# Attention scores from two 128-row matmuls, and running products times differences of values

## The chip, the cores and the metric

The kernel runs on one core of one Trainium2 chip. The metric is the device time of one execution in microseconds; before the change it is 1440.06 us (median of three runs, 1440.01 to 1440.62).

## What is computed

One decoder block over 1024 tokens of width 1024, all in float32: a norm and one wide input projection; two token mixers (an attention without softmax, and a gated linear attention, GLA); their gated merge and output projection; a gated feed-forward net with a short convolution; a last norm. The change lies in the attention, which has 8 heads of 64:

```python
z = einsum('bhqd,bhkd->bhqk', qb, kb) * scale          # scale = 64 ** -0.5
strict = s_idx < t_idx
log_keep = where(strict, log_sigmoid(-z), 0.0)
tail = cumsum(log_keep, reverse=True) - log_keep       # over the keys right of s
w = where(strict, exp(log_sigmoid(z) + tail), 0.0)
out = einsum('bhqk,bhkd->bhqd', w, vb)
```

In words: for a query t, each key s < t has a share b = sigmoid(z) and keeps 1 - b = sigmoid(-z). The weight of s is its b times the product of what all keys between s and t keep. With K(s) the product of sigmoid(-z) over the keys from s up to t - 1 (and K = 1 from t on), the weight of s is K(s + 1) - K(s).

## The kernel before

Matrix products in float32 are made of matmuls in a rounded type (fp32r): each operand is split into a high part, rounded, and a low part, the rest, by the helper `split` (line 118): a cast on ScalarE (ACT, line 119) and a subtraction on VectorE (DVE, line 110). `mac` (line 189) multiplies high by high, high by low and low by high; its matmuls have line 195. DVE's products have line 113 and its sums line 116, as these too are helpers.

The order of the instructions on each engine is set when the kernel is built: a scheduler takes the program's instructions by priority, which is their order in the program, when their inputs and buffers are ready by its own model of time. All engines work through their queues in order. Tiles come from pools with a fixed number of buffers: `t8` (128 x 2048, 16 buffers), `t4` (128 x 1024, 14), `t2` (128 x 512, 11), and 8 PSUM banks of 128 x 512.

The projections of the queries and keys lie in DRAM as `sqk_d` (a row for each of the 512 query and 512 key channels, a column for each token), the values as `sbv_d` (a row for each token).

`attend` (line 670) goes over four pairs of heads (j), over four groups of 256 queries (tp), over the two heads of the pair (e), over the two blocks of 128 queries in the group (i), and over the keys up to the block in chunks of at most 512 (four blocks of 128), the rightmost chunk first. That is 96 chunks in all. Each chunk goes through three steps, with up to six chunks queued between the first and the second:

- `weigh` (line 623): scores z of 128 queries by up to 512 keys in two matmuls. The first (line 631) has 128 rows: the high part of the 64 query channels and their low part below it, against the high part of the keys, doubled. The second (line 632) has 64 rows: the high part of the queries against the low part of the keys. ACT then makes sigmoid(z) (`be`, line 634) and sigmoid(-z) (`ke`, line 635). In a block's first chunk, GpSimd (POOL) masks both on the diagonal (line 638); in the others it multiplies the last column of `be` by the product that the chunk to the right left (line 643). DVE makes the running product of `ke` from the right (a scan, line 646), and multiplies `be` by it, moved by one column (line 648, seen as line 113).
- `turn_weights` (line 651): transposes the weights `be` in blocks on TensorE (line 654) and splits them.
- `gather` (line 657), when a group of queries is through: the values, in high and low parts side by side in 128 columns, times the weights' parts (line 663). The two halves of the result are added (a copy on ACT, line 666, and a sum on DVE), and the sum is stored to `osb_d` from SyncE's queue (SP).

`qk(j, t)` (line 562) prepares a pair: 11 loads on SP's queue, then in four steps the casts (lines 578 and 581) and subtractions (579 and 582). Pair 0 is prepared ahead of `attend`; the next pair from the last group of queries (tp = 3) of the current one on, a step after each chunk. `value_blocks` (line 613) loads and splits the value blocks in pairs during pair 0.

In between stand the matmuls of the merge gates (`gates`, line 524, seen as line 195). They need nothing from the attention; they have a lower priority, and `fill` hands out a step of six after every 3.6 key blocks or so.

Of the kernel before, what the change touches and what calls it, by code (L numbers as in the profile page):

```python
# [3 lines left out]

# [6 lines left out]
F32 = mybir.dt.float32  # L11
F32R = mybir.dt.float32r
AF = mybir.ActivationFunctionType
ALU = mybir.AluOpType
# [3 lines left out]
P = 128  # L18
D = 1024
S = 1024  # L20
NT = S // P
NK = D // P
HALF = 512
SBH, SBD = 8, 64
# [41 lines left out]
def block_kernel(ctx: ExitStack, tc: tile.TileContext, x, norm_mix_g, w_in, b_gate, w_alpha_up, b_alpha,  # L66
# [20 lines left out]
    def t8(dt=F32R):  # L87
        return sb.tile([P, 2 * D], dt, tag="t8", name=nm("t8"), bufs=16)

    def t4(dt=F32):  # L90
        return sb.tile([P, D], dt, tag="t4", name=nm("t4"), bufs=T4)

    def t2(dt=F32):
        return sb.tile([P, HALF], dt, tag="t2", name=nm("t2"), bufs=T2)

    def bank():
        return ps.tile([P, HALF], F32, tag="bank", name=nm("bank"), bufs=8)
# [4 lines left out]
    def by(a, k):  # L102
        return a.rearrange("p (k c) -> p k c", k=k)
# [5 lines left out]
    def sub(o, a, b):  # L109
        nc.vector.tensor_tensor(out=o, in0=a, in1=b, op=ALU.subtract)  # L110

    def mul(o, a, b):
        nc.vector.tensor_tensor(out=o, in0=a, in1=b, op=ALU.mult)  # L113
# [4 lines left out]
    def split(h, l, src):  # L118
        nc.scalar.copy(h, src)  # L119
        sub(l, src, h.bitcast(F32))  # L120
# [43 lines left out]
    def fill(steps, n):  # L164
        for _ in range(n):
            next(steps, None)
# [392 lines left out]

    HALVES = slice(0, 64), slice(64, 128)  # L560

    def qk(j, t):

        sq, kh, kl, raw = by(t8(), 2), by(t8(), 2), t4(F32R), t4()
        t += sq, kh, kl
        qr, kr = slice(j * P, (j + 1) * P), slice(HALF + j * P, HALF + (j + 1) * P)
        nc.sync.dma_start(kl.bitcast(F32), sqk_d[kr, :])
        for e in range(2):
            h = slice(j * P + e * 64, j * P + e * 64 + 64)
            other = HALVES[1 - e]  # L570
            nc.sync.dma_start(raw[other], sqk_d[h, :])
            for a in HALVES:
                nc.sync.dma_start(sq[a, e].bitcast(F32), sqk_d[h, :])
                nc.sync.dma_start(kh[a, e].bitcast(F32), sqk_d[slice(HALF + h.start, HALF + h.stop), :])
        for e in range(2):
            yield
            own, other = HALVES[e], HALVES[1 - e]
            nc.scalar.copy(sq[:, e], sq[:, e].bitcast(F32))
            sub(sq[other, e], raw[other], sq[other, e].bitcast(F32))
            yield  # L580
            nc.scalar.copy(kh[:, e], kh[:, e].bitcast(F32))
            sub(kl[own], kl[own].bitcast(F32), kh[own, e].bitcast(F32))

    def whole21():

# [12 lines left out]
    for n, _ in enumerate(steps):  # L598
        if n > 0 and n % 2 == 0:
            fill(side, 1)  # L600
        if n == 2 * len(pairs) - 1:
            fill(side, 9)
            del xq["s2"]
            q0 = []
            fill(qk(0, q0), 9)
            fill(gate_steps, 1)
    for a in ("s1", "s4"):
        del xq[a]
    again = whole21()

    vt = []

    def value_blocks(n):

        while len(vt) < n:
            v2 = t8().rearrange("p (b h d) -> p b h d", b=2, h=SBH)
            for i in (len(vt), len(vt) + 1):
                raw = t2()
                nc.sync.dma_start(raw, sbv_d[i * P:(i + 1) * P, :])
                split(v2[:, i % 2, :, 0:SBD], v2[:, i % 2, :, SBD:P], raw.rearrange("p (h d) -> p h d", h=SBH))  # L620
            vt.extend((v2[:, 0], v2[:, 1]))

    def weigh(t, e, i, b0, b1, right):

        sq, kh, kl = t
        own = HALVES[e]
        w = (b1 - b0) * P
        z = bank()
        cs = slice(b0 * P, b1 * P)
        ts_ = slice(i * P, (i + 1) * P)  # L630
        nc.tensor.matmul(z[:, 0:w], sq[:, e, ts_], kh[:, e, cs], start=True, stop=False)  # L631
        nc.tensor.matmul(z[:, 0:w], sq[own, e, ts_], kl[own, cs], start=False, stop=True)  # L632
        be, ke = t2(), t2()
        nc.scalar.activation(be[:, 0:w], z[:, 0:w], AF.Sigmoid, scale=SBD ** -0.5)  # L634
        nc.scalar.activation(ke[:, 0:w], z[:, 0:w], AF.Sigmoid, scale=-SBD ** -0.5)
        if right is None:
            for a, fill_ in ((be, 0.0), (ke, 1.0)):
                nc.gpsimd.affine_select(out=a[:, w - P:w], in_=a[:, w - P:w], pattern=[[-1, P]],  # L638
                                        compare_op=ALU.is_gt, fill=fill_, base=0, channel_multiplier=1)
            initial = 1.0  # L640
        else:
            initial = right[:, 0:1]
            nc.gpsimd.tensor_scalar(out=be[:, w - 1:w], in0=be[:, w - 1:w], scalar1=initial, scalar2=0.0,
                                    op0=ALU.mult, op1=ALU.add)
        kr = ke[:, 0:w][:, ::-1]
        nc.vector.tensor_tensor_scan(out=kr, data0=kr, data1=zero.to_broadcast([P, w]), initial=initial,  # L646
                                     op0=ALU.mult, op1=ALU.add)
        mul(be[:, 0:w - 1], be[:, 0:w - 1], ke[:, 1:w])
        return be, ke

    def turn_weights(be, nb, ah, al):
        pt = bank()
        for b in range(nb):
            nc.tensor.transpose(pt[:, b * P:(b + 1) * P], be[:, b * P:(b + 1) * P], ident)  # L654
        split(ah, al, by(pt[:, 0:nb * P], nb))

    def gather(head, tp, ah, al):
        po = bank()
        nb = 2 * tp + 2
        for b in range(nb):  # L660
            c0 = 0 if b < nb - 1 else P
            for n, a in enumerate((ah, al)):
                nc.tensor.matmul(po[:, c0:2 * P], vt[b][:, head, :], a[b // 4][:, b % 4, c0:],  # L663
                                 start=(b == 0 and n == 0), stop=(b == nb - 1 and n == 1))
        o = by(t2(), 2)
        nc.scalar.copy(o[0:64, 1], po[64:128, 0:2 * P])
        add(o[0:64, 0], po[0:64, 0:2 * P], o[0:64, 1])
        nc.sync.dma_start(osb_d[head * 64:(head + 1) * 64, tp * 2 * P:(tp + 1) * 2 * P], o[0:64, 0])

    def attend():  # L670

        todo, late = deque(), deque()

        def flush():
            *a, end = todo.popleft()
            turn_weights(*a)
            if end is not None:
                late.append(end)

        nxt, chunk = q0, 0  # L680
        for j in range(SBH // 2):
            t, nxt, coming = nxt, [], iter(())
            for tp in range(NT // 2):
                if tp == NEXT[j > 0] and j + 1 < SBH // 2:
                    coming = qk(j + 1, nxt)
                for e in range(2):
                    ng = (2 * tp + 2 + 3) // 4
                    ah, al = ([by(t4(F32R), 4) for _ in range(ng)] for _ in range(2))
                    for ii in range(2):
                        i = 2 * tp + ii  # L690
                        nb = i + 1
                        right = None
                        for b0, b1 in ([(0, nb)] if nb <= 4 else [(4, nb), (0, 4)]):
                            while len(todo) == AHEAD or sum(d[1] for d in todo) > BLOCKS:
                                if len(late) > LATE:
                                    gather(*late.popleft())
                                flush()
                            be, right = weigh(t, e, i, b0, b1, right)
                            fill(coming, 1)
                            if j == 0:  # L700
                                chunk += 1
                                if chunk >= AGAIN and (chunk - AGAIN) % EVERY == 0:
                                    fill(again, 1)
                                if chunk >= 2:
                                    fill(gate_steps, MORE * (chunk < 8))
                                    value_blocks(2 * tp + 2)
                            g = b0 // 4
                            d = [a[g][:, 0:b1 - b0, ii * P:(ii + 1) * P] for a in (ah, al)]
                            end = (2 * j + e, tp, ah, al) if ii == 1 and b0 == 0 else None
                            todo.append((be, b1 - b0, *d, end))  # L710
                            yield b1 - b0
        while todo:
            flush()
            while late:
                gather(*late.popleft())
            yield 2

    owed = 0
    for w in attend():
        owed += w + EACH  # L720
# [531 lines left out]
```

## Time and profile before

| | |
|---|---|
| median of the runs | 1440.06 us |
| the profiled execution | 1439.48 us |
| its span, first to last instruction | 1437.7 us |
| mean granted TensorE clock | 0.998 |
| attention, first score matmul to last gather | about 311 to 573 us |

Times in the profile are microseconds from the first instruction, unless marked ns. PE is TensorE's matmul, PEld its weight load, which may run beside the matmul before; SP is SyncE, whose queue issues most loads. A line of a group names the line of the kernel, the engine, the operation, the tiles and shapes and the count, then busy time in us and mean ns of one, then how long the engine was idle just before and what ended that. A matmul's written duration reaches over the start of the next, as matmuls are pipelined; the time that it takes from the engine is read from start to start. In a row of the view by stretch, each engine has its busy time and its count of instructions in brackets; the last three numbers are TensorE's granted clock, the share of DMA and GB/s.

### The profile page before, as it was taken

The numbers are of one execution on the slowest core, as the hardware profiler recorded it, in microseconds if no ns is written. First come the engines' busy times: TensorE is split into PE (matmuls) and PEld (weight loads), VectorE is DVE, ScalarE is ACT, GpSimd is POOL, SyncE is SP. The second block draws the span as 40 slices with busy tenths as digits, with TensorE's granted clock in tenths as the row PEclk, the third lists the DMA queues.
The fourth block names the chain that finished last, engine by engine and source line by source line (L and its number), as shares of the span: only waits on it lengthen the run. The fifth ranks groups of instructions, "written<-read, shape, count | busy, mean of one in ns | idle before, by whom it ended". The sixth has DMA issues, their size and how long they took to land.

```text
span 1437.7 us, 18652 instructions
## 1 busy us (share of the span) xinstructions
PE 1414.9 (98%) x6569; PEld 1146.1 (80%) x6569; DVE 1101.8 (77%) x1737; ACT 680.0 (47%) x1310; POOL 151.4 (11%) x277
## 2 busy tenths in 40 slices
PE   7999999999999999999999999999999999999997
PEld 6788888877777777878888788888888888888886
DVE  6397667858988977655744998998988887897755
ACT  6235433747867655471332643333333333554554
POOL 0000000012442432210000000010000000000000
PEclk9999999999999999999999999999999999999999
DMA  6332333467524424756242524664444437953332
GB/s 245 128 108 74 104 113 105 140 206 204 145 76 120 130 63 141 240 172 214 102 149 85 161 74 133 204 217 164 161 141 153 159 104 253 327 196 103 96 103 103
DMA packets 156798, 212.67 MB, mean 148 GB/s; under 512 B 9713, under 2 KB 102963, under 8 KB 156192
## 3 DMA queue, kind: packets, MB, share of 16 engines
q1 hardware_dynamic: 138096, 155.44, 35.5%
q0 software_dynamic: 11312, 41.48, 7.6%
q10 hardware_dynamic: 7296, 14.55, 2.7%
q8 instruction: 52, 0.85, 0.2%
q14 instruction: 42, 0.34, 0.1%
HBM read 153.64 MB, written 57.80 MB: 147 GB/s over the span
## 4 chain that ended last, share of the span: by engine, by line
PE 94%; DVE 3%; ACT 1%; DMA 1%; issue 1%; SPq 0%; DVEq 0%; ACTq 0%
PE bank L195 56%; PE bank L1115 15%; PE bank L366 6%; PE bank L982 5%; PE bank L663 2%; PE bank L654 2%; PE bank L632 2%; DVE t L110 2%; PE bank L631 1%; PE bank L319 1%; DVE t L116 1%; DMA t<-sqk_d 1%; PE bank L426 1%; PE bank L788 1%; PE bank L751 0%
## 5 line engine op out<-in xcount | busy, mean ns | idle before, releaser
L195 PE MATMUL bank<-t,t 128*128 128x512 f32 x3648 | 870.8, 394 | 0.9 <-DVE t L110 0.8
L195 PEld LDWEIGHTS bank<-t,t 128*128 128x128 f32 x3648 | 678.9, 188 | 155.7 <-issue 10.2
L110 DVE TENSOR_TENSOR t<-t,t 128x512 fp32r<-128x512 f32 (+1 forms) x659 | 438.2, 697 | 86.5 <-ACT t L119 77.9
L119 ACT CAST t<-t 128x512 fp32r<-128x512 f32 x537 | 311.4, 620 | 303.9 <-DVE t L110 67.2
L116 DVE TENSOR_TENSOR t<-bank,t 128x512 f32<-128x512 f32 (+1 forms) x284 | 182.5, 652 | 118.4 <-PE bank L195 69.0
L1115 PE MATMUL bank<-t,t 128*128 128x512 f32 x924 | 209.6, 389 | 0.0
L1115 PEld LDWEIGHTS bank<-t,t 128*128 128x128 f32 x924 | 173.4, 188 | 36.0
L113 DVE TENSOR_TENSOR t<-t,t 128x511 f32<-128x511 f32 (+5 forms) x134 | 92.6, 696 | 1.8 <-ACT t L513 0.8
L366 PE MATMUL bank<-t,t 128*128 128x512 f32 x384 | 91.4, 396 | 0.0
L982 PE MATMUL bank<-t,t 128*128 128x512 f32 x384 | 88.9, 391 | 0.0
L1013 ACT ACTIVATE t<-t,vcol 128x1024 f32<-128x1024 f32 x22 | 27.4, 1244 | 128.0 <-DVE t L116 128.0
L110 DVE TENSOR_TENSOR t<-bank,t 128x512 fp32r<-128x512 f32 (+4 forms) x128 | 72.3, 575 | 20.0 <-ACT t L119 19.9
L366 PEld LDWEIGHTS bank<-t,t 128*128 128x128 f32 x384 | 72.4, 191 | 15.5 <-DVE t L110 0.4
L982 PEld LDWEIGHTS bank<-t,t 128*128 128x128 f32 x384 | 71.6, 188 | 14.7
L116 DVE TENSOR_TENSOR t<-t,t 128x512 f32<-128x512 f32 x107 | 70.0, 684 | 16.1 <-ACT t L471 15.3
L110 DVE TENSOR_TENSOR t<-t 128x512 f32<-128x512 f32 x116 | 78.3, 683 | 3.6 <-DMA t<-in_w_ffn_in_dram 3.2
L119 ACT CAST t<-bank 128x512 fp32r<-128x512 f32 (+3 forms) x124 | 61.7, 512 | 38.9 <-PE bank L319 19.2
L638 POOL TENSOR_SCALAR_AFFINE_SELECT t<-t 128x128 f32<-128x128 f32 x128 | 65.9, 533 | 123.5 <-ACT t L634 118.3
L1015 DVE SCALAR_TENSOR_TENSOR t<-t,vcol,t 128x1023 f32<-128x1023 f32 (+1 forms) x44 | 56.2, 1277 | 14.1 <-ACT t L1013 13.9
L646 DVE TENSOR_TENSOR_SCAN t<-t,zero 128x128 f32<-128x128 f32 (+1 forms) x64 | 52.4, 822 | 15.8 <-POOL t L638 15.6
L634 ACT ACTIVATE t<-bank 128x128 f32<-128x128 f32 (+3 forms) x96 | 48.2, 502 | 16.7 <-PE bank L632 14.7
L654 PE MATMUL bank<-ident,t 128*128 128x128 f32 x288 | 49.7, 278 | 1.6 <-ACT t L634 0.8
(125 smaller groups left out, 864.0 us busy)
## 6 DMA issues: line engine op xcount, KB each, us to landing
t<-in_w_ffn_in_dram SPq DMA_DIRECT2D x50, 512.0 KB, 4.8
t<-in_w_in_dram SPq DMA_DIRECT2D x43, 512.0 KB, 5.2
act_d<-t POOLq DMA_DIRECT2D x22, 512.0 KB, 5.9
t<-in_w_ffn_out_dram SPq DMA_DIRECT2D x22, 512.0 KB, 6.8
wsum_d<-t POOLq DMA_DIRECT2D x22, 512.0 KB, 4.5
t<-act_d SPq DMA_DIRECT2D x22, 512.0 KB, 6.1
t<-wsum_d SPq DMA_DIRECT2D x44, 256.0 KB, 3.1
t<-sqk_d SPq DMA_DIRECT2D x40, 256.0 KB, 5.7
```

The lines of the kernel that those rows point to most:

```text
L110: nc.vector.tensor_tensor(out=o, in0=a, in1=b, op=ALU.subtract)
L113: nc.vector.tensor_tensor(out=o, in0=a, in1=b, op=ALU.mult)
L116: nc.vector.tensor_tensor(out=o, in0=a, in1=b, op=ALU.add)
L119: nc.scalar.copy(h, src)
L195: nc.tensor.matmul(pt, a[:, kk], b[:, kk], start=start and kk == 0 and m == 0, stop=stop and kk == k - 1 and m == 2)
L366: nc.tensor.matmul(pt, a[:, k % 4, t], b, start=k == 0 and m == 0, stop=k == NK - 1 and m == 2)
L638: nc.gpsimd.affine_select(out=a[:, w - P:w], in_=a[:, w - P:w], pattern=[[-1, P]], compare_op=ALU.is_gt, fill=fill_, base=0, channel_multi ...
L646: nc.vector.tensor_tensor_scan(out=kr, data0=kr, data1=zero.to_broadcast([P, w]), initial=initial, op0=ALU.mult, op1=ALU.add)
L654: nc.tensor.transpose(pt[:, b * P:(b + 1) * P], be[:, b * P:(b + 1) * P], ident)
L982: nc.tensor.matmul(pt, a[:, k % 4, t], b, start=(k == 0 and m == 0), stop=(k == NK - 1 and m == 2))
L1015: nc.vector.scalar_tensor_tensor(out=cv[:, i:], in0=av[:, :S - i], scalar=col(V_CW, (2 - i) * NF + f), in1=cv[:, i:], op0=ALU.mult, op1=AL ...
L1115: nc.tensor.matmul(pts[m][i], a[:, t], b, start=(k == 0 and x_ == 0), stop=(k == NH - 1 and x_ == 2))
```

## The change

- The low parts move from the queries to the keys. `keys` makes one operand `kk`: for each head the high part of the keys in one half of the partitions and the low part in the other. `queries` makes the queries doubled in both halves, once as their high part and once as their low part, for 512 tokens at a time: the first half of the tokens together with the keys, the second half (`th` = 1) at the start of the pair's own sweep. Both score matmuls then have 128 rows and the same moving operand.
- `weigh` makes only sigmoid(-z) and its running product `ke`. The weights, and with them the first sigmoid, its mask, the product with the last column and the product on DVE, are gone. What is transposed and split is the running product itself.
- The sum over the keys of (K(s + 1) - K(s)) v(s) is written as the sum of K(s) (v(s - 1) - v(s)), plus the value at the end of the block of queries. `value_blocks` therefore loads each block a second time, moved by one row, and subtracts on POOL; `last_values` loads the eight last rows, transposes them and keeps them in `vend`; `gather` adds them as a bias in two activations where there was one copy.

```diff
-    def qk(j, t):
-        sq, kh, kl, raw = by(t8(), 2), by(t8(), 2), t4(F32R), t4()
...
+    def keys(j, t):
+        kk, raw = by(t8(), 2), t4()
+        t.append(kk)
         for e in range(2):
+            h = slice(HALF + j * P + e * 64, HALF + j * P + e * 64 + 64)
+            nc.sync.dma_start(raw[HALVES[1 - e]], sqk_d[h, :])
+            for a in HALVES:
+                nc.sync.dma_start(kk[a, e].bitcast(F32), sqk_d[h, :])
+        for e in range(2):
+            yield
+            other = HALVES[1 - e]
+            nc.scalar.copy(kk[:, e], kk[:, e].bitcast(F32))
+            yield
+            sub(kk[other, e], raw[other], kk[other, e].bitcast(F32))
+
+    def queries(j, th, t):
+        q = by(t8(), 2)
+        t.append(q.rearrange("p a (e c) -> p a e c", e=2))
+        for a in HALVES:
+            nc.sync.dma_start(by(q[a, 1].bitcast(F32), 2),
+                              sqk_d[j * P:(j + 1) * P, th * HALF:(th + 1) * HALF].rearrange("(e p) c -> p e c", p=64))
+        yield
+        nc.scalar.copy(q[:, 0], q[:, 1].bitcast(F32))
+        yield
+        sub(q[:, 1], q[:, 1].bitcast(F32), q[:, 0].bitcast(F32))
...
+    vend = t2()[0:SBD, 0:SBH * NT]
+    def last_values():
+        raw = t2()
+        nc.sync.dma_start(raw[0:NT], sbv_d.rearrange("(n p) c -> p n c", p=P)[P - 1])
+        pt = bank()
+        for h in range(SBH):
+            nc.tensor.transpose(pt[0:SBD, h * NT:(h + 1) * NT], raw[0:NT, h * SBD:(h + 1) * SBD], ident[0:NT, 0:NT])
+        nc.vector.tensor_copy(vend, pt[0:SBD, 0:SBH * NT])
...
-                raw = t2()
+                raw, d = t2(), t2()
                 nc.sync.dma_start(raw, sbv_d[i * P:(i + 1) * P, :])
-                split(v2[:, i % 2, :, 0:SBD], v2[:, i % 2, :, SBD:P], raw.rearrange("p (h d) -> p h d", h=SBH))
+                if i == 0:
+                    nc.gpsimd.memset(d[0:1], 0.0)
+                    nc.sync.dma_start(d[1:P], sbv_d[0:P - 1, :])
+                else:
+                    nc.sync.dma_start(d, sbv_d[i * P - 1:(i + 1) * P - 1, :])
+                nc.gpsimd.tensor_tensor(out=d, in0=d, in1=raw, op=ALU.subtract)
+                split(v2[:, i % 2, :, 0:SBD], v2[:, i % 2, :, SBD:P], d.rearrange("p (h d) -> p h d", h=SBH))
...
-        nc.tensor.matmul(z[:, 0:w], sq[:, e, ts_], kh[:, e, cs], start=True, stop=False)
-        nc.tensor.matmul(z[:, 0:w], sq[own, e, ts_], kl[own, cs], start=False, stop=True)
-        be, ke = t2(), t2()
-        nc.scalar.activation(be[:, 0:w], z[:, 0:w], AF.Sigmoid, scale=SBD ** -0.5)
+        for a in range(2):
+            nc.tensor.matmul(z[:, 0:w], q[:, a, e, ts_], kk[:, e, b0 * P:b1 * P], start=a == 0, stop=a == 1)
+        ke = t2()
         nc.scalar.activation(ke[:, 0:w], z[:, 0:w], AF.Sigmoid, scale=-SBD ** -0.5)
...
-            nc.gpsimd.tensor_scalar(out=be[:, w - 1:w], in0=be[:, w - 1:w], scalar1=initial, scalar2=0.0,
-                                    op0=ALU.mult, op1=ALU.add)
...
-        mul(be[:, 0:w - 1], be[:, 0:w - 1], ke[:, 1:w])
-        return be, ke
+        return ke
...
-        nc.scalar.copy(o[0:64, 1], po[64:128, 0:2 * P])
+        for n in range(2):
+            c = slice(n * P, (n + 1) * P)
+            nc.scalar.activation(o[0:64, 1, c], po[64:128, c], AF.Identity,
+                                 bias=vend[:, head * NT + 2 * tp + n:head * NT + 2 * tp + n + 1])
...
+                if tp == 0:
+                    coming = queries(j, 1, t)
                 if tp == NEXT[j > 0] and j + 1 < SBH // 2:
-                    coming = qk(j + 1, nxt)
+                    coming = chain(keys(j + 1, nxt), queries(j + 1, 0, nxt))
...
+    last_values()
     owed = 0
     for w in attend():
```

More of the change, by code (lines that the diff above doesn't have):

```diff
@@ L2 @@
 from collections import deque
-from itertools import islice
+from itertools import chain, islice
 import concourse.bass as bass
@@ L560, in block_kernel @@
     HALVES = slice(0, 64), slice(64, 128)
-    def qk(j, t):
-        sq, kh, kl, raw = by(t8(), 2), by(t8(), 2), t4(F32R), t4()
-        t += sq, kh, kl
-        qr, kr = slice(j * P, (j + 1) * P), slice(HALF + j * P, HALF + (j + 1) * P)
-        nc.sync.dma_start(kl.bitcast(F32), sqk_d[kr, :])
+    def keys(j, t):
+        kk, raw = by(t8(), 2), t4()
+        t.append(kk)
         for e in range(2):
-            h = slice(j * P + e * 64, j * P + e * 64 + 64)
-            other = HALVES[1 - e]
-            nc.sync.dma_start(raw[other], sqk_d[h, :])
+            h = slice(HALF + j * P + e * 64, HALF + j * P + e * 64 + 64)
+            nc.sync.dma_start(raw[HALVES[1 - e]], sqk_d[h, :])
             for a in HALVES:
-                nc.sync.dma_start(sq[a, e].bitcast(F32), sqk_d[h, :])
-                nc.sync.dma_start(kh[a, e].bitcast(F32), sqk_d[slice(HALF + h.start, HALF + h.stop), :])
+                nc.sync.dma_start(kk[a, e].bitcast(F32), sqk_d[h, :])
         for e in range(2):
             yield
-            own, other = HALVES[e], HALVES[1 - e]
-            nc.scalar.copy(sq[:, e], sq[:, e].bitcast(F32))
-            sub(sq[other, e], raw[other], sq[other, e].bitcast(F32))
+            other = HALVES[1 - e]
+            nc.scalar.copy(kk[:, e], kk[:, e].bitcast(F32))
             yield
-            nc.scalar.copy(kh[:, e], kh[:, e].bitcast(F32))
-            sub(kl[own], kl[own].bitcast(F32), kh[own, e].bitcast(F32))
+            sub(kk[other, e], raw[other], kk[other, e].bitcast(F32))
[9 more added lines that the diff above has]
+        sub(q[:, 1], q[:, 1].bitcast(F32), q[:, 0].bitcast(F32))
     def whole21():
@@ L604, in block_kernel @@
             q0 = []
-            fill(qk(0, q0), 9)
+            for v in (keys(0, q0), queries(0, 0, q0)):
+                fill(v, 9)
             fill(gate_steps, 1)
@@ L621, in value_blocks @@
+                nc.gpsimd.tensor_tensor(out=d, in0=d, in1=raw, op=ALU.subtract)
+                split(v2[:, i % 2, :, 0:SBD], v2[:, i % 2, :, SBD:P], d.rearrange("p (h d) -> p h d", h=SBH))
             vt.extend((v2[:, 0], v2[:, 1]))
     def weigh(t, e, i, b0, b1, right):
-        sq, kh, kl = t
-        own = HALVES[e]
+        kk, q = t[0], t[1 + i // 4]
         w = (b1 - b0) * P
         z = bank()
-        cs = slice(b0 * P, b1 * P)
-        ts_ = slice(i * P, (i + 1) * P)
-        nc.tensor.matmul(z[:, 0:w], sq[:, e, ts_], kh[:, e, cs], start=True, stop=False)
@@ L632, in weigh @@
-        nc.tensor.matmul(z[:, 0:w], sq[own, e, ts_], kl[own, cs], start=False, stop=True)
-        be, ke = t2(), t2()
-        nc.scalar.activation(be[:, 0:w], z[:, 0:w], AF.Sigmoid, scale=SBD ** -0.5)
+        ts_ = slice(i % 4 * P, (i % 4 + 1) * P)
+        for a in range(2):
+            nc.tensor.matmul(z[:, 0:w], q[:, a, e, ts_], kk[:, e, b0 * P:b1 * P], start=a == 0, stop=a == 1)
+        ke = t2()
         nc.scalar.activation(ke[:, 0:w], z[:, 0:w], AF.Sigmoid, scale=-SBD ** -0.5)
         if right is None:
[L637 to L643, printed above, removed]
-                                    op0=ALU.mult, op1=ALU.add)
@@ L645, in weigh @@
-        kr = ke[:, 0:w][:, ::-1]
-        nc.vector.tensor_tensor_scan(out=kr, data0=kr, data1=zero.to_broadcast([P, w]), initial=initial,
-                                     op0=ALU.mult, op1=ALU.add)
-        mul(be[:, 0:w - 1], be[:, 0:w - 1], ke[:, 1:w])
-        return be, ke
-    def turn_weights(be, nb, ah, al):
+            nc.gpsimd.affine_select(out=ke[:, w - P:w], in_=ke[:, w - P:w], pattern=[[-1, P]],
+                                    compare_op=ALU.is_gt, fill=1.0, base=0, channel_multiplier=1)
@@ L652, in turn_weights @@
+        kr = ke[:, 0:w][:, ::-1]
+        nc.vector.tensor_tensor_scan(out=kr, data0=kr, data1=zero.to_broadcast([P, w]),
+                                     initial=1.0 if right is None else right[:, 0:1], op0=ALU.mult, op1=ALU.add)
+        return ke
+    def turn_weights(ke, nb, ah, al):
         pt = bank()
         for b in range(nb):
-            nc.tensor.transpose(pt[:, b * P:(b + 1) * P], be[:, b * P:(b + 1) * P], ident)
+            nc.tensor.transpose(pt[:, b * P:(b + 1) * P], ke[:, b * P:(b + 1) * P], ident)
@@ L697, in attend @@
                                 flush()
-                            be, right = weigh(t, e, i, b0, b1, right)
+                            right = weigh(t, e, i, b0, b1, right)
                             fill(coming, 1)
@@ L709, in attend @@
                             end = (2 * j + e, tp, ah, al) if ii == 1 and b0 == 0 else None
-                            todo.append((be, b1 - b0, *d, end))
+                            todo.append((right, b1 - b0, *d, end))
                             yield b1 - b0
```

## The prediction

> **What bounds the kernel now.** I read the engine table and the chain that ended last first.
>
> ```profile
> span 1437.7 us, 18652 instructions
> PE 1414.9 (98%) x6569; PEld 1146.1 (80%) x6569; DVE 1101.8 (77%) x1737; ACT 680.0 (47%) x1310; POOL 151.4 (11%) x277
> PE 94%; DVE 3%; ACT 1%; DMA 1%; issue 1%; SPq 0%; DVEq 0%; ACTq 0%
> ```
>
> TensorE is busy for 98% of the span and carries 94% of the chain. An average can hide a stage with another limit, so the next view is busy time by stretch: the attention runs from the first score matmul to the last gather, 311 to 573 us.
>
> ```profile
> core 0: us, PE busy (x) PEld busy (x) DVE busy (x) ACT busy (x) POOL busy (x), PEclk, DMA share, GB/s
> 311.00:573.00 262.00, 260.38 (x1327) 197.32 (x1326) 228.72 (x371) 180.07 (x393) 91.13 (x160) 1.00 0.44 125
> ```
>
> PE has work in 260.4 of these 262 us at full clock; VectorE is second with 228.7 (87%). So work taken from DVE, ACT or POOL here is worth nothing by itself, and work taken from PE is worth its full time, provided the others keep up. But a busy PE need not be a PE at its peak rate. The timeline of PE shows the rate from start to start.
>
> ```profile
> 426.18 0.42 PE L631 MATMUL bank<-t,t 128*128 128x384 f32 x1
> 426.52 0.44 PE L632 MATMUL bank<-t,t 64*128 64x384 f32 x1
> 426.89 1.43 PE L195 MATMUL bank<-t,t 128*128 128x512 f32 x5
> ...
> 428.51 0.48 PE L631 MATMUL bank<-t,t 128*128 128x512 f32 x1
> 428.92 0.49 PE L632 MATMUL bank<-t,t 64*128 64x512 f32 x1
> 429.34 0.66 PE L654 MATMUL bank<-ident,t 128*128 128x128 f32 x4
> 429.75 0.47 PE L631 MATMUL bank<-t,t 128*128 128x512 f32 x1
> 430.16 0.50 PE L632 MATMUL bank<-t,t 64*128 64x512 f32 x1
> 430.59 1.67 PE L195 MATMUL bank<-t,t 128*128 128x512 f32 x6
> ...
> 572.67 6.82 PE L195 MATMUL bank<-t,t 128*128 128x512 f32 x29
> 579.33 0.59 PE L751 MATMUL bank<-t,t 128*128 128x256 f32 x2
> ```
>
> 29 matmuls of 512 columns in a row take 579.33 - 572.67 = 6.66 us, 0.23 us each: the native rate. Of the score pair (L631 with 128 rows, L632 with 64), L632 starts 0.41 us after L631, and what follows starts 0.42 to 0.43 us after L632. Each of the two costs almost two native matmuls. The weight loads say when:
>
> ```profile
> 428.92 0.18 PEld L632 LDWEIGHTS bank<-t,t 64*128 64x128 f32 x1 [0.25 <-issue]
> 429.34 0.42 PEld L654 LDWEIGHTS bank<-ident,t 128*128 128x128 f32 x4 [0.24 <-issue]
> ```
>
> The weights of L632 load only as L632 starts, after 0.25 us in which the loader waited for nothing recorded, and so do the weights of the next 128-row matmul, after 0.24 us. Every entry into and exit from the 64-row form empties the pipeline. It isn't the shared bank: the 29 matmuls above accumulate a dozen and more to a bank and run at 0.23.
>
> **The change, part by part.** (1) *The second score matmul gets 128 rows.* The number of matmuls is unchanged; both are 128-row, and the two pipeline gaps go. How many of each width there are:
>
> ```profile
> L632 PE MATMUL bank<-t,t x96: 323/466/502, 311.1 to 557.8; 64*128 64x512 f32 x48, 64*128 64x128 f32 x16, 64*128 64x256 f32 x16, 64*128 64x384 f32 x16
> ...
> 438.04 0.31 PE L631 MATMUL bank<-t,t 128*128 128x128 f32 x1
> 438.27 0.32 PE L632 MATMUL bank<-t,t 64*128 64x128 f32 x1
> 438.52 0.96 PE L195 MATMUL bank<-t,t 128*128 128x512 f32 x3
> ...
> 441.54 0.36 PE L631 MATMUL bank<-t,t 128*128 128x256 f32 x1
> 441.83 0.38 PE L632 MATMUL bank<-t,t 64*128 64x256 f32 x1
> 442.14 0.33 PE L631 MATMUL bank<-t,t 128*128 128x128 f32 x1
> ```
>
> Width 512: 0.41 + 0.425 now, 2 x 0.23 after, 0.375 saved, x48 = 18.0 us. Width 384: 0.34 + 0.37 now, 2 x 0.1725 (0.23 scaled by the columns), 0.365 saved, x16 = 5.8. Width 256: 0.29 + 0.31 now, 2 x 0.115, 0.37 saved, x16 = 5.9. Width 128: 0.23 + 0.25 now; after, 0.10 each, the rate of the 128-column transposes (four in 0.41 us, 429.34 to 429.75), 0.28 saved, x16 = 4.5. Sum 34.2 us. If only the delay ahead of the 64-row matmul went and the one behind it had another cause, it would be about half, 17 us; nothing in the rows supports a second cause, so I take 34.2.
>
> (2) *Running products instead of weights.* These groups go or shrink:
>
> ```profile
> L113 DVE TENSOR_TENSOR t<-t,t 128x127 f32<-128x127 f32 (+3 forms) x96 | 53.0, 554 | 0.7
> L634 ACT ACTIVATE t<-bank 128x128 f32<-128x128 f32 (+3 forms) x96 | 48.2, 502 | 16.7 <-PE bank L632 14.7 <-POOL t L638 1.3 <-ACT t L635 0.2
> L638 POOL TENSOR_SCALAR_AFFINE_SELECT t<-t 128x128 f32<-128x128 f32 x128 | 65.9, 533 | 123.5 <-ACT t L634 118.3 <-ACT t L635 4.4 <-PE bank L195 0.2
> L643 POOL TENSOR_SCALAR t<-t,t 128x1 f32<-128x1 f32 x32 | 25.7, 804 | 69.9 <-ACT t L634 33.1 <-DVE t L646 11.3 <-ACT t L635 8.7
> L666 ACT COPY t<-bank 64x256 f32<-64x256 f32 x32 | 11.8, 369 | 11.5 <-PE bank L663 7.3 <-issue 3.2 <-DVE t L110 0.4
> L635 ACT ACTIVATE t<-bank 128x128 f32<-128x128 f32 x16 | 4.7, 292 | 0.0
> ```
>
> DVE loses all 96 products of line 648 (53.0 us). ACT loses the 96 first sigmoids (48.2) and gains the split of L666 in two with a bias: two of 0.29 (the nearest shape, 128x128 from a bank) for one of 0.37, 32 times, +6.9. POOL loses half of its selects (33.0) and all of L643 (25.7). All of it lies beside PE: 0 us. The cover is PE's own 228 us or so after the change, beside DVE's 228.7 - 53.0 = 175.7 (77%, less than the 87% now), ACT's 180.1 - 41.3 = 138.8 (61%) and POOL's 91.1 - 58.7 plus part (3). Without that cover each engine's share would matter, but all three fall further than PE does. The way from score to transpose also gets shorter, by a sigmoid, a select and a product.
>
> (3) *Differences of values.* Eight blocks get a second load and a POOL subtraction of 128x512 with two inputs, which has no row. From below:
>
> ```profile
> L780 POOL TENSOR_SCALAR_AFFINE_SELECT t<-t 128x512 f32<-128x512 f32 x8 | 5.0, 637 | 18.9 <-ACT t L779 10.4 <-DMA t<-gr_d 8.4
> t<-sqk_d SPq DMA_DIRECT2D x40, 256.0 KB, 5.7
> t<-sbv_d SPq DMA_DIRECT2D x8, 256.0 KB, 3.7
> ```
>
> One input at that size took 0.64 us; four times the 0.533 us of a 128x128 select is 2.1 us from above. I take 1.4 (the shape is that of the first, the operands are double), 11 us in all on an engine that falls to about 43 of 229 us. On the path: 0, as the value blocks have several chunks before the first gather; the bound above is the third rival. The Trainium skill (GPSIMD Engine Reference, the table of measured `tensor_tensor` times) gives 4497 ns for 2048 columns, which scaled to 512 is an estimate of 1.1 us; POOL's sum would be 9 us by it and the total the same.
>
> (4) *Preparation of a pair.* 11 loads of sqk_d become 10 of 256 KB: six for the keys, four for the queries, two of which move to the start of the pair's own sweep. Casts stay at four a pair, of 1024 columns, and the subtractions at four. On SP they stand, as now, between the stores of the outputs. 0 us, if they are in time: the second half of the queries is asked for at the first chunk and needed eight chunks later.
>
> (5) *last_values.* One load, eight small transposes, one copy, once. Eight at 0.10 us plus two changes of form at 0.19 (0.42 - 0.23): +1.2 us. From below 0 (hidden while PE waits), from above one load landing, 3.7 us, plus these, 4.9.
>
> Sum: -34.2 + 1.2 = -33.0 us. The profiled execution took 1439.48 us, 1.8 us around its span of 1437.7 and 0.6 below the median of the runs, 1440.06. So 1439.5 - 33.0 = 1406.5 against the profiled run, and 1440.1 - 33.0 = **1407 us** against the median; its own range, with 17 to 36 us saved (34.2 and the 1.6 us that PE now sits idle) and 0 to 4.9 us for part (5), is 1404 to 1428.
>
> **The rivals.** *Part of the gain is given back at the pairs.* The tiles of 128x2048 a pair needs rise from two to three, of 16 shared with the projected inputs and the values, so the next pair's keys or queries may be loaded only when the current pair lets go. Late is then: a load (5.7), a cast, a subtraction, a sigmoid, a scan and four transposes:
>
> ```profile
> L634 ACT ACTIVATE t<-bank 128x512 f32<-128x512 f32 x48 | 29.2, 609 | 8.7 <-PE bank L632 8.5
> L578 ACT CAST t<-t 128x1024 fp32r<-128x1024 f32 x6 | 6.4, 1074 | 5.5 <-DMA t<-sqk_d 5.5
> L110 DVE TENSOR_TENSOR t<-t,t 64x1024 fp32r<-64x1024 f32 x16 | 19.3, 1214 | 2.2 <-ACT t L578 1.9
> L646 DVE TENSOR_TENSOR_SCAN t<-t,t,zero 128x512 f32<-128x512 f32 x32 | 40.8, 1276 | 2.7 <-ACT t L635 2.7
> ```
>
> 5.7 + 1.1 + 1.2 + 0.6 + 1.3 + 0.4 = 10.3 us, three times, 31 us if PE had nothing else. For it: ACT waits 5.5 us for sqk_d already now. Against it: PE has gate matmuls and the gathers of queued chunks to run meanwhile. With half covered, 1407 + 15 = 1422 us.
>
> *The rows are not what costs.* The Trainium skill (TensorE: Matmul & The Clock Gate, Part 2, on LDWEIGHTS) says that time goes with the columns and that the row count doesn't matter; by that rule 64 rows to 128 gives nothing. As a mechanism of this kernel: the score pair would keep 0.41 + 0.42 us, PE its 262 us, and the time would be 1440 + 1.2, about 1441 us. Against it stands that of 1327 matmuls in the stretch the delayed ones are L632 and those right behind it. The same skill's TensorEngine Tiling (Array Packing), Key Properties, has a change of tiling mode drain the engine, which is how the rows look.
>
> *Slower: POOL holds up the scans.* The eight subtractions stand in POOL's order among the selects of the first pair, and each waits for two loads. A select behind one waits, and with it the scan on DVE and the transposes on PE, in order. Price: 3.7 + 2.1 = 5.8 us a block, 46 us for eight, 1453 us; from 33 / 8 = 4.1 us a block that reaches PE the kernel is slower than before. For it: DVE's scan waits for POOL's selects already. Against it: POOL is idle most of the time, and in the first 60 us PE has 145 gate matmuls as cover (the row is PE's and its loader's share of line 195):
>
> ```profile
> 311.00:371.00 60.00, 39.12 (x145) 26.03 (x144) 1.00 0.64 185
> ```
>
> **How the numbers follow.** The forecast 0.68; 1422 us 0.17; no gain 0.05; slower 0.05; and 0.05 that still more is gained (PE's idle time and waits shrink too), 1400. Between runs, 0.2% (2.9 us) is about what can be told from no change. Faster 0.68 + 0.17 + 0.05 = 0.90, same or near it 0.04 of the no-gain case, slower 0.05 + 0.01 = 0.06. The range goes from 1400 to 1426 us: it takes in nearly all of the own range, the first rival and the larger gain, and leaves out the two at and above 1440.
>
> **What would show it.** After: no 64-row form on the score line; the second score matmul 0.23 us after the first, its weights loaded ahead; no issue wait of the loader there; about 229 us from the first score matmul to the last gather, DVE near 176 us and ACT near 139 in it; PE idle below 3 us. Wrong would be: starts still 0.41 apart (rows not the cause); PE waiting for ACT's casts of keys or queries at the three pair starts, or for scans behind POOL in the first pair; an output bias that makes ACT load tables; or a stretch that shrinks while the stages behind it grow.

## The result and the profile after

The changed kernel takes 1416.72 us (median of four runs, 1415.16 to 1418.35) against 1440.03 us: 0.9839 of the time before, 95% interval 0.9822 to 0.9856. It gained 23.3 us where 33 were forecast. The head of its page:

```profile
span 1414.7 us, 18378 instructions
PE 1383.0 (98%) x6577; PEld 1143.1 (81%) x6577; DVE 1061.3 (75%) x1642; ACT 650.7 (46%) x1246; POOL 108.2 (8%) x190
```

PE's busy time fell from 1414.9 to 1383.0, by 31.9 us, close to the forecast. The span fell by only 23.0. PE's idle time rose from 22.8 us (1437.7 - 1414.9) to 31.7: 8.9 us were given back as waits. The view by stretch says where. First the kernel before, in the attention's first pair of heads and after it (columns as in the prediction):

```profile
311.00:373.00 62.00, 60.80 (x286) 44.81 (x284) 54.16 (x88) 48.06 (x100) 21.04 (x36) 1.00 0.63 180
373.00:550.00 177.00, 176.58 (x908) 133.65 (x908) 157.87 (x259) 118.95 (x267) 66.02 (x117) 1.00 0.38 105
```

Then the changed kernel:

```profile
311.00:373.00 62.00, 51.88 (x275) 40.85 (x274) 45.16 (x64) 39.01 (x81) 23.25 (x24) 1.00 0.69 207
373.00:550.00 177.00, 176.96 (x1061) 153.66 (x1060) 141.15 (x210) 110.83 (x247) 24.50 (x49) 1.00 0.42 121
```

From 373 us on PE never stops, and gets through 1061 matmuls in 177 us where it did 908. In the first 62 us it sits idle for 10.1 us, against 1.2 before. In this stretch the new kernel makes the differences of the values. Its matmuls and then its weight loads, in order of time:

```profile
437.89 0.47 PE L195 MATMUL bank<-t,t 128*128 128x512 f32 x1
438.20 0.39 PE L654 MATMUL bank<-t,t 128*128 128x512 f32 x1
438.43 0.39 PE L195 MATMUL bank<-t,t 128*128 128x512 f32 x1
438.66 0.40 PE L654 MATMUL bank<-t,t 128*128 128x512 f32 x1
438.90 2.44 PE L195 MATMUL bank<-t,t 128*128 128x512 f32 x10
...
437.98 0.19 PEld L654 LDWEIGHTS bank<-t,t 128*128 128x128 f32 x1
438.21 0.19 PEld L195 LDWEIGHTS bank<-t,t 128*128 128x128 f32 x1
438.43 0.19 PEld L654 LDWEIGHTS bank<-t,t 128*128 128x128 f32 x1
```

Line 654 now holds both score matmuls. At 512 columns each takes 0.23 to 0.24 us from start to start, as a gate matmul does, and its weights load about 0.2 us ahead, during the matmul before. The 0.41 and 0.42 us and the loader's waits are gone.

Where the 10 us went is told by the waits between 311 and 373 us (who waited, for whom, us in total, times, longest):

```profile
POOL t L643 <- DMA t<-sbv_d: 15.2, 4, 4.9
ACT t L119 <- POOL t L643: 11.8, 7, 3.2
DVE t L661 <- POOL t L658: 10.7, 6, 5.7
...
PE bank L677 <- ACT t L119: 1.9, 1, 1.9
```

and by single instructions of that stretch in order of time (POOL, ACT and PE put together from their timelines):

```profile
321.66 1.30 POOL L643 TENSOR_TENSOR t<-t,t 128x512 f32<-128x512 f32 x1 [4.93 <-DMA t<-sbv_d]
...
322.99 0.62 ACT L119 CAST t<-t 128x512 fp32r<-128x512 f32 x1 [3.23 <-POOL t L643]
...
324.50 1.66 ACT L119 CAST t<-t 128x512 fp32r<-128x512 f32 x3 [0.88 <-POOL t L643]
...
325.69 0.50 PE L195 MATMUL bank<-t,t 128*128 128x512 f32 x1 [0.65 <-ACT t L119]
...
329.00 2.24 POOL L643 TENSOR_TENSOR t<-t,t 128x512 f32<-128x512 f32 x1 [0.69 <-DVE t L110]
...
331.27 0.62 ACT L119 CAST t<-t 128x512 fp32r<-128x512 f32 x1 [2.05 <-POOL t L643]
331.80 0.37 ACT L119 CAST t<-bank 128x256 fp32r<-128x256 f32 x1
...
332.22 0.39 PE L677 MATMUL bank<-t,t 128*128 128x256 f32 x1 [1.93 <-ACT t L119]
```

POOL's subtraction (line 643) waits for a load of the values; the cast of the difference stands in ACT's order and waits for POOL; behind that cast stand the casts of gate weights (two of the three from 324.50) and of transposed blocks (331.80, read from a bank), and PE waits for those. It is a chain of three queues, each in order, that starts at a late load. Of the 10.1 us that PE waits in this stretch, 2.6 end with such a cast of line 119 and 4.0 with a subtraction of VectorE (line 110), which follows the casts; 1.3 end with the cast of reloaded inputs (line 598) and 1.2 with a scan. That is a reading of one trace; the runs below test it.

Why the first load is late stands in the same trace. SP issues the four loads of the first two blocks one after the other:

```profile
301.58 3.23 SPq L637 DMA_DIRECT2D t<-sbv_d  x1
304.99 0.25 SPq L640 DMA_DIRECT2D t<-sbv_d  x1
305.36 4.85 SPq L637 DMA_DIRECT2D t<-sbv_d  x1
310.25 0.59 SPq L642 DMA_DIRECT2D t<-sbv_d  x1
```

The first, of 128 rows, lands 7.7 us after its issue. The second (line 640) is the moved load of block 0. It has 127 rows, as nothing stands ahead of row 0, and POOL can start only at 321.66, 16.7 us after its issue. The two behind it land 16.7 and 12.5 us after theirs. A row of the values moves as a packet of 2048 bytes: from 311 to 313 us 51 to 73 of them start on this queue in each half microsecond, from 313 to 320 us only 2 to 9. So this load was not asked for late, it moved slowly. That the 127 rows are the reason is likely, as the packets of the 128-row loads around it come faster; no run changes that alone.

### The profile page after: what moved, and what is told of

Same layout as the page of the kernel before. It is cut to its first block, busy times and chain, and to the rows that moved or that the text cites. A ratio compares the mean times of both kernels' runs of the same rounds, so it can differ in the third digit from the quotient of the medians.

```text
span 1414.7 us, 18378 instructions
## 1 busy us (share of the span) xinstructions
PE 1383.0 (98%) x6577; PEld 1143.1 (81%) x6577; DVE 1061.3 (75%) x1642; ACT 650.7 (46%) x1246; POOL 108.2 (8%) x190
## 4 chain that ended last, share of the span: by engine, by line
PE 70%; DVE 2%; ACT 1%; issue 0%; DVEq 0%; ACTq 0%
PE bank L195 42%; PE bank L1135 15%; PE bank L1002 5%; PE bank L677 2%; PE bank L654 2%; PE bank L668 2%; DVE t L110 1%; DVE t L116 1%; PE bank L808 1%; PE bank L771 0%; PE bank L843 0%; PE bank L795 0%; PE bank L820 0%; PE bank L319 0%; DVE t L311 0%
## 5 line engine op out<-in xcount | busy, mean ns | idle before, releaser
L110 DVE TENSOR_TENSOR t<-t,t 128x512 fp32r<-128x512 f32 (+2 forms) x651 | 430.3, 694 | 83.3 <-ACT t L119 78.1
L110 DVE TENSOR_TENSOR t<-t 128x512 f32<-128x512 f32 (+1 forms) x124 | 88.0, 718 | 5.3 <-DMA t<-in_w_ffn_in_dram 3.5
L654 PE MATMUL bank<-t,t 128*128 128x128 f32 (+3 forms) x192 | 55.7, 368 | 1.6 <-DVE t L110 1.6
L658 POOL TENSOR_SCALAR_AFFINE_SELECT t<-t 128x128 f32<-128x128 f32 x64 | 34.2, 540 | 192.2 <-ACT t L656 184.0
L677 PE MATMUL bank<-t,t 128*128 128x256 f32 (+1 forms) x320 | 45.8, 277 | 2.7 <-ACT t L119 1.9
```

The lines of the kernel that those rows point to most:

```text
L654: nc.tensor.matmul(z[:, 0:w], q[:, a, e, ts_], kk[:, e, b0 * P:b1 * P], start=a == 0, stop=a == 1)
```

## The experiments

**The two halves apart.** The first run puts only the second score matmul of the kernel before on 128 rows:

```diff
-        nc.tensor.matmul(z[:, 0:w], sq[own, e, ts_], kl[own, cs], start=False, stop=True)
+        nc.tensor.matmul(z[:, 0:w], sq[:, e, ts_], kl[:, cs], start=False, stop=True)
```

> The kernel before with one line changed: the second score matmul takes all 128 rows of the operands that it has (the other 64 rows multiply the low part of the queries with the low part of the other head's keys, a rounding-sized term that is added). Theory (every entry into and exit from the 64-row form empties TensorE's pipeline): 34 us less, about 1406 us, the two score matmuls 0.23 us apart at 512 columns. Rival (rows do not matter, the gain of the changed kernel comes from the running products): 1440 us, starts still 0.41 us apart.

Measured: 1419.77 us, 0.9853 (0.9838 to 0.9868). The rows do matter, but 21 us came instead of 34. Its stretches:

```profile
311.00:373.00 62.00, 57.61 (x311) 47.22 (x309) 57.36 (x92) 51.07 (x106) 24.88 (x39) 1.00 0.66 189
373.00:550.00 177.00, 170.43 (x1004) 145.09 (x1004) 170.60 (x280) 127.92 (x287) 69.77 (x121) 1.00 0.41 115
```

What PE waited for most between 311 and 552 us:

```profile
PE bank L654 <- DVE t L113: 6.1, 6, 1.2
```

PE is idle for 4.4 and 6.6 us, and VectorE is busy for 170.6 of the 177 us, 96%. PE waits for line 113, the product that makes the weights. So with the rows alone the bound passes from TensorE to VectorE. The next run takes that product away and keeps all else:

```diff
-        mul(be[:, 0:w - 1], be[:, 0:w - 1], ke[:, 1:w])
```

> The run with only the second score matmul on 128 rows, now without the product on VectorE after the scan (the transposed weights are then the sigmoids alone, so another sum is computed). Theory (with only the rows changed TensorE's stream became as short as VectorE's 228 us, so VectorE took over 13 us of the 34): VectorE falls to about 175 us in the attention, 1407 to 1410 us. Rival (the first sigmoids on ScalarE, the selects on GpSimd or the way through one chunk hold it up): 1417 to 1420 us as with the rows alone.

Measured: 1411.52 us, 0.9797 (0.9782 to 0.9812), 8 us less, a little short of what was expected. Its stretches:

```profile
311.00:373.00 62.00, 55.58 (x286) 45.58 (x286) 44.85 (x68) 46.78 (x98) 16.98 (x37) 0.97 0.61 180
373.00:550.00 177.00, 176.57 (x1055) 152.73 (x1054) 139.17 (x208) 131.65 (x298) 60.08 (x124) 1.00 0.44 127
```

And PE's longest wait in the first of these:

```profile
PE bank L195 <- ACT t L592: 2.8, 1, 2.8
```

After 373 us VectorE falls to 139 us and PE's idle time from 6.6 to 0.4: VectorE was the bound there, and the sigmoids and selects that this run still has were not. The 6.4 us of idle time in the first pair have another cause; the longest wait is for the cast of reloaded inputs (line 592). That part isn't settled.

The other half alone is the changed kernel with its second score matmul on 64 rows:

```diff
-            nc.tensor.matmul(z[:, 0:w], q[:, a, e, ts_], kk[:, e, b0 * P:b1 * P], start=a == 0, stop=a == 1)
+            r = HALVES[e] if a else slice(0, P)
+            nc.tensor.matmul(z[:, 0:w], q[r, a, e, ts_], kk[r, e, b0 * P:b1 * P], start=a == 0, stop=a == 1)
```

> The changed kernel with its second score matmul on 64 rows again (the low part of the queries against the high part of the keys, the product of the two low parts left out). Theory: the pipeline gaps come back, 30 to 34 us, 1441 to 1450 us: 1450 if the 9 us of waits in the first pair stay, 1441 if the slower stream hides them. Rival (the gain is the running products'): 1417 us.

Measured: 1444.47 us, 1.0024 (1.0015 to 1.0034). 27.8 us come back; the running products at the old rate save nothing, and with the differences made in the first pair the kernel is about 4 us slower than before.

**What the differences cost.** The changed kernel with its value blocks made as before:

```diff
-                raw, d = t2(), t2()
+                raw = t2()
                 nc.sync.dma_start(raw, sbv_d[i * P:(i + 1) * P, :])
...
-                nc.gpsimd.tensor_tensor(out=d, in0=d, in1=raw, op=ALU.subtract)
-                split(v2[:, i % 2, :, 0:SBD], v2[:, i % 2, :, SBD:P], d.rearrange("p (h d) -> p h d", h=SBH))
+                split(v2[:, i % 2, :, 0:SBD], v2[:, i % 2, :, SBD:P], raw.rearrange("p (h d) -> p h d", h=SBH))
```

> The changed kernel with the value blocks made as before: one load each, no subtraction on GpSimd (the differences of the values are left out, so another sum is computed). Theory (the 9 us that came short of the forecast are waits for the differences in the first pair): TensorE idle about 1 us between 311 and 373 us, 1408 us. Rival (they come from the shorter stream itself or from the reload of the projected inputs): 1416 us, TensorE idle still near 10 us there.

Measured: 1407.47 us, 0.9768 (0.9754 to 0.9783), 9.2 us less than the changed kernel. In the first pair PE's idle time falls from 10.1 to 2.3 us:

```profile
311.00:373.00 62.00, 59.73 (x330) 49.44 (x328) 50.16 (x76) 45.50 (x94) 10.80 (x17) 1.00 0.62 184
```

The same kernel with the second score matmul on 64 rows again (both edits above together) closes the square:

> The changed kernel without the differences of the values (one load for each block, no subtraction, so another sum is computed) and with the second score matmul on 64 rows. With it the two halves of the change stand alone and together, without the cost of making the differences: 1441 us before, 1420 us with the rows alone, this one, 1407 us with both. Theory (at the old rate TensorE's stream covers what the running products take from the other engines): 1439 to 1441 us. Rival (the running products are worth 12 us by themselves, as the step from 1420 to 1407 looks): 1428 us.

Measured: 1440.20 us, 0.9992 (0.9983 to 1.0002), no difference from before. The four, without the cost of the differences, in us:

| | weights, three engines loaded | running products |
|---|---|---|
| second matmul on 64 rows | 1440 to 1442 | 1440.2 |
| second matmul on 128 rows | 1419.8 | 1407.5 |

The products are worth nothing at 64 rows and 12 us at 128; the rows 21 us with the weights and 33 with the products.

**Which part of making the differences.** One load for each block, and a POOL operation of the same shape on it:

```diff
-                if i == 0:
...
-                nc.gpsimd.tensor_tensor(out=d, in0=d, in1=raw, op=ALU.subtract)
+                nc.gpsimd.tensor_tensor(out=d, in0=raw, in1=raw, op=ALU.add)
```

> The changed kernel with one load for each value block and a GpSimd operation of the same shape on it (the block is added to itself instead of the difference, so another sum is computed). Theory 1 (the second load, and what waits for it, makes the 9 us): 1408 to 1410 us. Theory 2 (GpSimd's operation in the way, with ScalarE's cast in order behind it): 1414 to 1417 us.

Measured: 1408.39 us, 0.9773 (0.9757 to 0.9789). So POOL's operation in the way costs about a microsecond (1408.4 against 1407.5, within the scatter), and the second load, with what waits for it, the other 8. The subtraction on VectorE instead, with both loads:

```diff
-                nc.gpsimd.tensor_tensor(out=d, in0=d, in1=raw, op=ALU.subtract)
+                sub(d, d, raw)
```

> The changed kernel with the eight subtractions on VectorE instead of GpSimd, both loads kept. Theory 1 (the late loads): 1413 to 1418 us, as changed or worse, since VectorE then waits in order for the loads. Theory 2 (GpSimd's operation, 1.3 to 3.1 us each, in the way): 1408 to 1411 us.

Measured: 1414.09 us, 0.9812 (0.9797 to 0.9827). Of the 9.2 us, 6.6 stay without POOL, in line with the loads. But the row of the first pair shows that two things lie in these 6.6 us:

```profile
311.00:373.00 62.00, 57.38 (x295) 46.90 (x294) 47.48 (x75) 42.09 (x85) 11.86 (x17) 0.94 0.68 208
```

PE's idle time falls from 10.1 to 4.6 us, while TensorE's granted clock falls to 0.94. So the time alone says less about the loads than it seems to. All eight blocks asked for ahead of the attention:

```diff
     last_values()
+    value_blocks(NT)
     owed = 0
```

> The changed kernel with all eight value blocks asked for ahead of the attention instead of group by group in the first pair. Theory (the waits come from loads asked for too late in the first pair): most of the 9 us come back, 1408 to 1411 us. Rival (the buffers and the engines' order ahead of the attention have no room, or the waits are GpSimd's own): 1415 us or more.

Measured: 1413.35 us, 0.9811 (0.9795 to 0.9828), between the two expectations. The waits are not gone but drawn together into two long ones at the start of the attention:

```profile
328.13 0.48 PE L668 MATMUL bank<-ident,t 128*128 128x128 f32 x1 [3.89 <-DVE t L661]
...
333.43 0.79 PE L195 MATMUL bank<-t,t 128*128 128x512 f32 x1 [4.19 <-ACT t L119]
```

Sixteen loads in a row need buffers just as the attention starts: SP's value loads wait 13.8 us for stores of gates (gate_d), whose `t2` buffers they take. And the moved load of block 0 is slow here too: it is issued at 301.38 us and its subtraction starts at 314.66; three of the loads behind it land 11.0 to 12.6 us after their issue. The second load issued by POOL instead of SP (two lines, `nc.sync` to `nc.gpsimd`):

> The changed kernel with the second load of each value block issued by GpSimd instead of SyncE. Theory 1 (the second load is late since it stands in SyncE's order behind loads that wait for buffers): about 1409 to 1412 us. Theory 2 (it is late since it waits for a buffer itself, whoever issues it): 1415 to 1418 us.

Measured: 1414.35 us, 0.9814 (0.9798 to 0.9830), again between the two; the interval overlaps that of the changed kernel (0.9822 to 0.9856). In its waits between 311 and 373 us:

```profile
POOL t L658 <- DMA t<-sqk_d: 7.6, 1, 7.6
POOL t L643 <- DMA t<-sbv_d: 4.9, 4, 2.0
```

POOL's wait for values falls from 15.2 to 4.9 us, while one of its selects is now recorded behind a load of sqk_d for 7.6. The moved load of block 0 lands 3.3 us after POOL issues it, so its slow landing is gone, and yet the time is only 2.4 us lower: that landing by itself doesn't make the 8 us, unless a new cost hides what it gives back. PE still waits once for 3.4 us for a cast of line 119, and the granted clock is 0.94 from 311 to 373 us. Whether the later loads are late for their place on SP or for want of a buffer stays open.

**The differences made elsewhere.** During the input projections of the changed kernel POOL is busy for 10.8 of 197 us:

```profile
114.00:311.00 197.00, 197.00 (x865) 160.10 (x863) 138.63 (x226) 92.19 (x145) 10.82 (x20) 1.00 0.40 118
```

There a difference is made, stored, and loaded in the attention as one block:

```diff
+    def difference(i):
+        raw, d = t2(), t2()
...
+        nc.gpsimd.tensor_tensor(out=d, in0=d, in1=raw, op=ALU.subtract)
+        nc.gpsimd.dma_start(dv_d[i * P:(i + 1) * P, :], d)
...
+        if 6 <= n < 6 + NT:
+            difference(n - 6)
...
-                raw, d = t2(), t2()
-                nc.sync.dma_start(raw, sbv_d[i * P:(i + 1) * P, :])
...
+                d = t2()
+                nc.sync.dma_start(d, dv_d[i * P:(i + 1) * P, :])
```

> The changed kernel with the eight differences made during the input projections, when GpSimd is nearly idle, and stored; in the attention each value block is one load again. Theory (all that the change lacks against the forecast is the making of the differences in the first pair): 1407 to 1409 us, as without differences, with the whole sum computed. Rival (the work only moves its waits into the projections): 1412 to 1418 us.

Measured: 1417.16 us, 0.9829 (0.9815 to 0.9844). The rival was right: the wait had moved. Between 150 and 200 us:

```profile
POOL t L613 <- DMA t<-sbv_d: 18.1, 1, 18.1
ACT t L487 <- DMA dv_d<-t: 14.3, 1, 14.3
...
PE bank L196 <- ACT t L119: 5.3, 1, 5.3
```

The first subtraction waits 18 us for the moved load of block 0, which is slow again (issued at 177.53 us; the subtraction starts at 192.21). An activation on ACT (line 487) takes a `t2` buffer and waits 14.3 us for the store of that first difference (dv_d); the casts of the next weights stand behind it in ACT's order, and PE waits 5.3 us for those. So what links POOL's wait to PE is a buffer and ACT's queue, not the stores of the projections behind POOL, as the next expectation has it. The loads are now asked for one step ahead, and the blocks spread over sixteen steps:

```diff
         nc.sync.dma_start(d, sbv_d[i * P - 1:(i + 1) * P - 1, :])
+        yield
         nc.gpsimd.tensor_tensor(out=d, in0=d, in1=raw, op=ALU.subtract)
...
-        if 6 <= n < 6 + NT:
-            difference(n - 6)
+        if 2 <= n < 2 + 2 * NT:
+            fill(ahead_of, 1)
```

> The differences made ahead, during the projections, with the loads of a block asked for one step of the projections before its subtraction, and spread over sixteen steps. Theory (the run with the differences ahead lost its gain to one wait of GpSimd for a first load, with the projections' stores in order behind it): no wait of TensorE there, 1408 to 1411 us. Rival (GpSimd's queue meets the loads too early again): 1414 to 1418 us.

Measured: 1407.20 us, 0.9758 (0.9744 to 0.9773): the whole computation at the time of the run without differences, and 9.5 us below the changed kernel. Projections and first pair:

```profile
114.00:311.00 197.00, 197.00 (x869) 159.88 (x868) 140.89 (x226) 91.92 (x145) 31.38 (x37) 1.00 0.51 154
...
311.00:373.00 62.00, 60.21 (x335) 50.26 (x333) 50.76 (x77) 46.18 (x97) 11.28 (x18) 1.00 0.63 186
```

PE doesn't stop in the 197 us of the projections, though POOL's load there triples from 10.8 us, and is idle for 1.8 us in the first pair. POOL still waits for loads there, 49.9 us in five waits; they just hold up nothing that PE needs. The step ahead, the earlier start and the spreading came together, so which of them did it isn't shown.

## Why the prediction was right, and where it was not

The direction and the mechanism held; the size was off by 9.7 us, and one step carries nearly all of that.

*Part (1), the rows: right.* Forecast 34.2 us. Between the two kernels that differ only in this matmul (on 64 rows it also leaves out the product of the two low parts), the time went from 1440.2 to 1407.5 us: 32.7, or 0.34 us for each of the 96 chunks. The rates taken for the narrower matmuls were a little low: at 256 columns the median is 0.14 us from start to start, not 0.115, at 384 columns 0.22, not 0.17. The price was read from starts in the timeline of PE; the busy times of the score lines would not have shown it, as a matmul's written duration of 0.4 to 0.5 us is long with and without the gap. By the Trainium skill (TensorE: Matmul & The Clock Gate, Part 2) the row count doesn't matter for the time of a weight load. The traces agree for the load itself, 0.18 us with 64 rows and 0.19 with 128. Carried over to the whole stream, as the rival did, it would have given no gain, and these 32.7 us are against that. The Trainium skill's TensorEngine Tiling (Array Packing), Key Properties, has a change of tiling mode drain the engine, and the trace agrees: the gaps went with the changes of form.

*Part (2), the running products at 0 us: right, for a reason that the step only half gave.* At the old rate they are worth nothing (0.9992). The step added that each engine's share would matter without that cover, and put VectorE at 175.7 us beside PE's 228. Unsaid was the other side: VectorE's 228.7 us as they were would have been as long as PE's new stream, so 12 of the 33 us hang on this half; VectorE's product alone accounts for 8.3 of them (1419.8 to 1411.5 us). Summing each half by itself, with 0 for the second, gives the right total only because both are there. The shares themselves were put too low: from 311 to 552 us VectorE is busy for 186.7 us and ACT for 151.2, not 176 and 139, and neither became the bound.

*Part (3), the differences at 0 us on the path: the step that failed.* It held that "the value blocks have several chunks before the first gather". The values were in time for the gather: in the first pair its matmuls wait 2.6 us in all, and those are waits for the split of a transposed block. What the step left out is what stands behind a difference in the queues. The cast of a difference stands in ACT's order ahead of casts that PE needs at once, and it waited for POOL, which waited for the load. Without the differences the time is 9.2 us lower, without the second load alone 8.3. The step had 3.7 us for a load of values to land; the moved load of block 0 took 16.7 until POOL could start. POOL's time for the operation was put at 1.4 us; its group in the attention shows

```profile
L643 POOL TENSOR_TENSOR t<-t,t 128x512 f32<-128x512 f32 x8 | 13.5, 1684 | 15.9 <-DMA t<-sbv_d 15.2 <-DVE t L110 0.7
L682 ACT ACTIVATE t<-bank,t 64x128 f32<-64x128 f32 x64 | 20.4, 361 | 18.0 <-PE bank L677 17.0 <-ACT t L656 0.4 <-PE bank L668 0.2
```

1.7 us as a mean, inside the two bounds, though two of the eight took 2.24 and 3.12 us, above the upper one. The estimate of 1.1 us from the Trainium skill (GPSIMD Engine Reference, the `tensor_tensor` times) was low by a third here. The split copy of the outputs (line 682) took 0.36 us a piece, not 0.29. On the path POOL's operation costs 0.9 us (1408.4 against 1407.5), within the scatter; for the copies no run shows a cost.

*Part (4), the loads of a pair: right.* From 373 us on PE is idle for 0.04 us, over three starts of a pair.

*Part (5), last_values: too high, without consequence.* The eight transposes took 0.35 us of PE (311.28 to 311.63, start to start) instead of 1.2.

*The rivals.* The first, loads that come late at the pairs, did not happen, though its 1422 us lies near the result: a like loss in another place. That the time lies in the stated range of 1400 to 1426 us is in part luck: it does so by the room made for this rival and for a smaller gain from the rows, neither of which came true. The slower rival had the right place, POOL's queue in the first pair, and a wrong price: 46 us if every block's wait reached PE, 8.9 as measured, which fits the cover by gate matmuls that it named. And it named only the selects behind POOL's subtraction: VectorE's scans did wait 10.7 us for them, but PE waited only 1.2 us for a scan, and ACT's casts were the other way through.

## What to carry to other kernels

Read a busy engine's rate from start to start; a change of the matmul's form inside a stream can cost nearly as much as a matmul (0.19 us beside 0.23 here), and it is in no group's duration. When the bound engine gets faster, add up the next engine's load against the new length: a relief that is worth nothing alone can be what lets the other through. And ask of each new instruction not only when its result is needed, but what stands behind it in its queue while it waits; here the new preparatory work cost nothing where its queues were idle and its loads were asked for a step ahead. Look, too, at when a load lands, and not only at when it is asked for.

## What was not expected

The granted clock of TensorE dropped in the first pair of some runs: to 0.83 as a mean from 311 to 341 us where all value blocks were asked for early (PE busy for 21.93 of 30 us, with waits of 3.9 and 4.2 us):

```profile
311.00:341.00 30.00, 21.93 (x102) 17.80 (x102) 20.85 (x26) 14.61 (x28) 14.54 (x16) 0.83 0.81 267
```

It dropped to 0.94 from 311 to 373 us in the run with the subtractions on VectorE, where PE's longest wait is 1.6 us. The changed kernel, with a longest wait of 1.9 us, kept 1.00 in the rows above. So the length of the longest wait alone doesn't decide it, and what does isn't settled here. A drop makes a wait cost more than its own length: in the run on VectorE six gate matmuls from 333.62 us on take 2.66 us, 0.44 each, where 0.23 is usual.

Also, POOL's subtraction of one shape took between 1.28 and 3.12 us within a kernel.
